# One trunk layer on one core: the first weight unit goes ahead of the next k-tiles' modulation products, and the square-root table is loaded later

## The chip, the cores and the metric

The kernel runs on one core of one Trainium2 chip. The metric is the device time of one execution in microseconds (us); lower is better. The engines are TensorE (PE for its matmuls, PEld for its weight loads), VectorE (DVE), ScalarE (ACT), GpSimd (POOL) and SyncE (SP, which here only issues DMAs).

## The reference

One layer of a diffusion trunk is applied to 128 context tokens and 256 latent tokens (384 rows of width 2048, float32). What matters here is its beginning and the place where the second half starts:

```python
sh1, sc1, g1, sh2, sc2, g2 = split(silu(cond) @ w_mod + b_mod, 6)   # one cond for context, one for latent
h  = rms_norm(x, n1) * (1 + sc1) + sh1
p  = h @ w_in                                   # 2048 -> 4096: q, k, v, u
...
x  = x + g1 * ((g_na * na + g_fn * fn) @ w_o)   # gates from h, attention and Fourier branches
h2 = rms_norm(x, n2) * (1 + sc2) + sh2
x  = x + g2 * (silu(b) * a) @ w_down            # a, b = split(h2 @ w_gate_up)
```

Each of the six pieces of the modulation is 2048 wide and needs a 2048 x 2048 part of `w_mod` (16.8 MB).

## The kernel before, in words

**Weight units.** All weights stream through one list of units, each of two k-tiles (256 rows) by 512 columns (512 KB), or one k-tile where a group has an odd one. `load_unit` (L179 on) issues the load on SyncE's queue into one of four buffers. `split_unit` makes a high part `wh` with a cast on ScalarE (L137) and a low part `wl` with a subtraction on VectorE (L138), into three buffers each, and TensorE multiplies with three matmuls for each product (`mm3`, L141 to L143). `next_unit` (L202) is called once for each unit, ahead of its matmuls: it splits a later unit, then gives one tick to every helper in the list `behind` (and to those in `front`, which get two there and one more from `mid_unit`), then issues another load.

**Helpers and rates.** A helper is a Python generator wrapped in `Paced` (L54). A tick adds its `rate` to `due`, and each whole 1 in `due` runs the generator on to its next `yield`, which I call a step. The engines' instructions are thus put into their queues in an order that these counts set. Each engine takes its own queue strictly in order; engines wait for each other by semaphores.

**The opening.** `x` is loaded, transposed and squared, and `mod_cols` (L358 on) makes shift and scale 1 in column form: it loads `w_mod` in chunks of 1 MB (tile `wm`, three buffers), multiplies each chunk with the conditions (32, 16 or 8 matmuls into tile `md`, at 128, 256 or 512 columns), and asks for the chunk three ahead. It does so for the k-tiles in the parts `MODS`: 0; 1 to 2; 3 to 6; 7 to 10; 11 to 14; 15. Then `modulate(kt)` (L520) makes `hH`, `hL` of one k-tile. The input projection runs in four groups (`GROUPS`), so that it can begin before all k-tiles are there: k-tile 0 alone, 1 to 2, 3 to 6, 7 to 15; in each, eight column chunks of 512 (8, 8, 16 and 40 units). All that comes after k-tile 0 is one helper, `prep` (L548 to L559): for a part of n k-tiles 2n chunk steps, 3 more (the last chunk's step also copies the products; one step does nothing, one turns them with matmuls at L405, one adds the bias at L415 to L418), and n steps of `modulate`. At the start of a group `prep.due` is set to `DUE` and its rate to `PREP` (L623):

```python
DUE = [0, -0.5, 0, 0]
PREP = [1.3, 1.8, 2.3, 2.3]
RATES = [1.455, 0.5, 1.1, 0.937, 0.452]
```

A group's matmuls also force `prep` on if the k-tile that they need has not been modulated yet (L632).

**The other four pieces.** When `prep` has ended, its `then` (L577) appends the helper `rows` to `behind`; its first tick comes with the next unit. `rows` (L562) makes pieces 2 (gate 1), 4 (scale 2), 3 (shift 2) and 5 (gate 2) in this order: multiply-adds on VectorE (L312, L314), then a sum over partitions with matmuls (L324), an addition of the bias on VectorE (`row`, L329), and four small stores from GpSimd's queue to DRAM (`s_row`, L334). For pieces 4 and 3 `columns` reads the row back as columns (`colr`, L340, two loads on GpSimd's queue), transposes it on TensorE (L347), and writes it to `msc[1]` or `msh[1]` on VectorE (L351 for shift 2). The rates of `rows` are those of `RATES`: 1.455 in the input projection, 0.5 for each of three ticks of a unit in the gate stage (64 units), 1.1 in the branch projections (32 units), 0.937 in the output projection, where it is set to 0 for the last two of 32 units. Where a piece must be there, `rows_until(ty)` (L573) runs the steps that are still missing, on the spot.

**The end of the output projection.** After its last unit the sums of squares are reduced and `inv_sqrt` runs (L1149 to L1152), then `rows_until(3)` (L1153), then TensorE transposes the reciprocal roots (L1157), ScalarE copies them (`rB`, L1159) and `normed` makes the first k-tiles of `h2` for the feed-forward stage.

**Activation tables.** `warm_sqrt` (L145) is a one-column square root, so that ScalarE loads the table of roots there and not where the real root (L157) waits.

Of the kernel before, what the change touches and what calls it, by code (L numbers as in the profile page):

```python
# [38 lines left out]
MODS = [(0, 1), (1, 2), (3, 4), (7, 4), (11, 4), (15, 1)]  # L39
GROUPS = MODS[:3] + [(7, 9)]  # L40
ORDER = [6, 7, 0, 1, 2, 3, 4, 5]
DUE = [0, -0.5, 0, 0]
PREP = [1.3, 1.8, 2.3, 2.3]
PAIR = "qk,b,pv,s0 m0,e0 i0,,s1 m1,e1 i1,,t0,v,,t1,,"
RATES = [1.455, 0.5, 1.1, 0.937, 0.452]
# [50 lines left out]
def trunk_kernel(ctx: ExitStack, tc: tile.TileContext, io: dict):  # L96
# [35 lines left out]
    def nm(s):  # L132
        return f"{s}{next(ids)}"
# [11 lines left out]
    def warm_sqrt():  # L145

        warm = small.tile([P, 1], F32, tag="warm", bufs=1, name=nm("warm"))
        nc.scalar.activation(out=warm, in_=ones[:, 0:1], func=AF.Sqrt)
# [112 lines left out]
    with ExitStack() as ph:  # L261
# [7 lines left out]
        def at_tile():  # L269
            return pa.tile([P, CH], F32, tag="at", name=nm("at"))  # L270
# [3 lines left out]
        def acc_tile():  # L274

            return next(ring)()
# [147 lines left out]
        with ExitStack() as pha:  # L424
# [4 lines left out]
            def c6(shape, name):  # L429
                return cpool.tile(shape, F32, tag="c6", name=nm(name))  # L430
# [39 lines left out]
            nc.scalar.activation(  # L470
                out=csz[:, :, 0:2], in_=pt[:, 0:32].rearrange("p (c k) -> p k c", c=2), func=AF.Silu
            )
            warm_sqrt()


            ssx = small.tile([P, NT, 4], F32, tag="ssx", bufs=1, name="ssx")
# [1 line left out]
            for cc in range(4):  # L478
                xT.append(c6([P, 4, TOK], "xT"))
                for k in range(4):  # L480
                    o = acc_tile()
                    for t in (1, 2, 0):
                        nc.tensor.transpose(o[:, t * P : (t + 1) * P], xc[cc][:, t, k * P : (k + 1) * P], ident)
                    nc.vector.tensor_copy(xT[cc][:, k], o[:, :TOK])
                for t in (1, 2, 0):
                    junk = tmp.tile([P, CH], F32, tag="junk", bufs=1, name=nm("junk"))
                    nc.scalar.activation(
                        out=junk, in_=xc[cc][:, t], func=AF.Square, accum_out=ssx[:, t, cc : cc + 1]
                    )
                if cc == 1:  # L490
                    pt = at_tile()
                    nc.tensor.transpose(pt[:, 0:64], rows_n, ident[:64, :64])
                    nc.vector.tensor_copy(ng, pt[:, 0:32].rearrange("p (i k) -> p i k", i=2))
                    nc.vector.tensor_copy(bcol, pt[:, 32:64])
                    nc.vector.tensor_scalar_mul(qg8, qg[:, 0:1], HD**-0.5)
            ss1 = small.tile([P, NT], F32, tag="ss1", bufs=1, name="ss1")
            nc.vector.tensor_reduce(out=ss1, in_=ssx, axis=AX.X, op=ALU.add)
            r1 = small.tile([P, NT], F32, tag="r1", bufs=1, name="r1")
# [123 lines left out]
            for gi, (k0, n) in enumerate(GROUPS):  # L622
                prep.due, prep.rate = DUE[gi], PREP[gi]  # L623
                if gi == len(GROUPS) - 1:
# [700 lines left out]
```

## Time and profile before

| | us |
|---|---|
| median of 3 runs | 2071.12 (2070.62 to 2074.38) |
| the profiled execution, its time | 2071.76 |
| its span, first to last instruction | 2070.0 |
| TensorE matmuls busy | 2035.2 (98%) |
| VectorE busy | 1225.5 (59%) |
| ScalarE busy | 758.2 (37%) |
| GpSimd busy | 43.2 (2%) |
| mean granted TensorE clock | 0.996 of full speed |

The profile is of one execution. Times in its rows count from the first instruction, so that 1.76 us of the execution lie outside the span. Busy time of TensorE runs on while a matmul waits in the pipeline; idle time before an instruction stands in brackets with the engine and line that released it. The page of the profile gives the whole execution in groups; the timeline gives the instructions of one engine in order of time, merged where neighbours are alike.

### The profile page before, as it was taken

The numbers are of one execution on the slowest core, as the hardware profiler recorded it, in microseconds if no ns is written. First come the engines' busy times: TensorE is split into PE (matmuls) and PEld (weight loads), VectorE is DVE, ScalarE is ACT, GpSimd is POOL, SyncE is SP. The second block draws the span as 40 slices with busy tenths as digits, with TensorE's granted clock in tenths as the row PEclk, the third lists the DMA queues.
The fourth block names the chain that finished last, engine by engine and source line by source line (L and its number), as shares of the span: only waits on it lengthen the run. The fifth ranks groups of instructions, "written<-read, shape, count | busy, mean of one in ns | idle before, by whom it ended". The sixth has DMA issues, their size and how long they took to land.

```text
span 2070.0 us, 27406 instructions
## 1 busy us (share of the span) xinstructions
PE 2035.2 (98%) x10986; PEld 1846.1 (89%) x10986; DVE 1225.5 (59%) x1454; ACT 758.2 (37%) x1133; POOL 43.2 (2%) x92
## 2 busy tenths in 40 slices
PE   7999999999999999998999999999999999999999
PEld 4658888999999999887998899899989998999897
DVE  5635899688986787765554444544454434333456
ACT  5323232456665443334433332223222232223222
POOL 1000000000001000001000000000000000000000
PEclk9999999999999999999999999999999999999999
DMA  9887878677774775754545554455454444444453
GB/s 329 297 318 218 298 247 315 209 211 232 213 223 150 255 245 198 244 182 133 153 153 163 157 159 153 136 160 162 154 163 133 125 130 127 128 126 128 130 166 122
DMA packets 219999, 390.45 MB, mean 189 GB/s; under 512 B 28080, under 2 KB 64960, under 8 KB 219872
## 3 DMA queue, kind: packets, MB, share of 16 engines
q1 hardware_dynamic: 212704, 382.13, 58.2%
q10 hardware_dynamic: 4672, 6.31, 0.8%
q8 instruction: 86, 1.41, 0.3%
q0 software_dynamic: 2496, 0.27, 0.1%
q14 instruction: 41, 0.34, 0.0%
HBM read 371.81 MB, written 20.51 MB: 190 GB/s over the span
## 4 chain that ended last, share of the span: by engine, by line
PE 89%; DVE 3%; DMA 3%; ACT 2%; issue 1%; SPq 1%; ACTq 0%; DVEq 0%
PE mm L141 18%; PE mm L143 18%; PE mm L142 18%; PE at L143 11%; PE at L141 11%; PE at L142 10%; PE md L392 1%; DMA wm<-in_w_mod 1%; DVE accr L314 1%; DMA wraw<-in_w_gate 1%; DVE wl L138 1%; ACT wh L137 0%; ACT sc L900 0%; SPq L368 0%; PE at L858 0%
## 5 line engine op out<-in xcount | busy, mean ns | idle before, releaser
L138 DVE TENSOR_TENSOR wl<-wraw,wh 128x1024 fp32r<-128x1024 f32 (+1 forms) x464 | 559.1, 1205 | 699.9 <-ACT wh L137 693.5
L137 ACT CAST wh<-wraw 128x1024 fp32r<-128x1024 f32 (+1 forms) x464 | 480.6, 1037 | 1030.3 <-PE at L142 283.5
L141 PE MATMUL mm<-hH,wh 128*128 128x384 f32 x1216 | 411.6, 338 | 3.6 <-ACT gst L998 2.5
L143 PE MATMUL mm<-hH,wl 128*128 128x384 f32 x1216 | 407.6, 335 | 0.0
L142 PE MATMUL mm<-hL,wh 128*128 128x384 f32 x1216 | 407.2, 335 | 0.0
L314 DVE SCALAR_TENSOR_TENSOR accr<-wmr,csz,accr 128x1024 f32<-128x1024 f32 x240 | 304.7, 1277 | 0.1
L141 PE MATMUL at<-hH,wh 128*128 128x384 f32 x704 | 236.6, 336 | 1.4 <-ACT hH L1170 1.4
L141 PEld LDWEIGHTS mm<-hH,wh 128*128 128x128 f32 x1216 | 228.9, 188 | 9.2 <-ACT gst L998 3.7
L142 PE MATMUL at<-hL,wh 128*128 128x384 f32 x704 | 236.4, 336 | 0.0
L143 PE MATMUL at<-hH,wl 128*128 128x384 f32 x704 | 235.9, 335 | 0.0
L142 PEld LDWEIGHTS mm<-hL,wh 128*128 128x128 f32 x1216 | 229.0, 188 | 0.0
L143 PEld LDWEIGHTS mm<-hH,wl 128*128 128x128 f32 x1216 | 228.7, 188 | 0.0
L141 PE MATMUL mm<-wh,hH 128*128 128x512 f32 x422 | 168.8, 400 | 1.8 <-DVE gl L1054 1.2
L142 PE MATMUL mm<-wl,hH 128*128 128x512 f32 x422 | 165.0, 391 | 0.9 <-DVE wl L138 0.9
L143 PE MATMUL mm<-wh,hL 128*128 128x512 f32 x422 | 164.7, 390 | 0.0
L143 PE MATMUL mm<-wh,cL 128*128 128x512 f32 x352 | 137.1, 389 | 0.0
L141 PE MATMUL mm<-wh,cH 128*128 128x512 f32 x352 | 137.0, 389 | 0.0
L142 PE MATMUL mm<-wl,cH 128*128 128x512 f32 x352 | 137.0, 389 | 0.0
L141 PEld LDWEIGHTS at<-hH,wh 128*128 128x128 f32 x704 | 132.7, 189 | 2.8 <-ACT hH L1170 1.8
L142 PEld LDWEIGHTS at<-hL,wh 128*128 128x128 f32 x704 | 132.7, 189 | 1.1 <-DVE hL L1176 0.7
L143 PEld LDWEIGHTS at<-hH,wl 128*128 128x128 f32 x704 | 132.7, 189 | 0.0
L141 PEld LDWEIGHTS mm<-wh,hH 128*128 128x128 f32 x422 | 79.5, 188 | 33.7 <-issue 11.1
(239 smaller groups left out, 2390.2 us busy)
## 6 DMA issues: line engine op xcount, KB each, us to landing
wraw<-in_w_gate_up SPq DMA_DIRECT2D x176, 512.0 KB, 3.7
wmr<-in_w_mod SPq DMA_DIRECT2D x128, 512.0 KB, 4.2
wraw<-in_w_down SPq DMA_DIRECT2D x88, 512.0 KB, 3.7
wm<-in_w_mod SPq DMA_DIRECT2D x64, 512.0 KB, 7.1
wraw<-in_w_gate SPq DMA_DIRECT2D x64, 512.0 KB, 5.0
wraw<-in_w_in SPq DMA_DIRECT2D x56, 512.0 KB, 5.8
wraw<-in_w_o SPq DMA_DIRECT2D x32, 512.0 KB, 5.5
wraw<-in_w_fnet_proj SPq DMA_DIRECT2D x16, 512.0 KB, 6.2
```

Of the source, the lines that this page charges most:

```text
L137: nc.scalar.copy(H, x)
L138: nc.vector.tensor_sub(L, x, fr(H))
L141: nc.tensor.matmul(out, aH, bH, start=start, stop=False)
L142: nc.tensor.matmul(out, aH, bL, start=False, stop=False)
L143: nc.tensor.matmul(out, aL, bH, start=False, stop=stop)
L314: nc.vector.scalar_tensor_tensor(out=acc[:, cnd], in0=wm, scalar=sc, in1=acc[:, cnd], op0=ALU.mult, op1=ALU.add)
L392: nc.tensor.matmul(pm[q : q + 32, :w], csz[:, k, :], wm[:, ty, kk + par, :], start=k < 2, stop=k >= KT - 2, tile_position=(0, q), skip_gro ...
```

## The change

`DUE` of the first group goes from 0 to -1.4, so that `prep` gets no step with the first unit and one step fewer in the first group. `warm_sqrt` moves from behind the SiLU of the conditions to behind the squares of the third column chunk of `x`. Nothing else differs.

```diff
-DUE = [0, -0.5, 0, 0]
+DUE = [-1.4, -0.5, 0, 0]
 PREP = [1.3, 1.8, 2.3, 2.3]
...
                 out=csz[:, :, 0:2], in_=pt[:, 0:32].rearrange("p (c k) -> p k c", c=2), func=AF.Silu
             )
-            warm_sqrt()
...
                     nc.vector.tensor_scalar_mul(qg8, qg[:, 0:1], HD**-0.5)
+                if cc == 2:
+                    warm_sqrt()
             ss1 = small.tile([P, NT], F32, tag="ss1", bufs=1, name="ss1")
```

## Rows read from the trace of the kernel before

**Rows 1.** The page, busy time, share of the span and instructions of TensorE.

```profile
PE 2035.2 (98%) x10986; PEld 1846.1 (89%) x10986; DVE 1225.5 (59%) x1454; ACT 758.2 (37%) x1133; POOL 43.2 (2%) x92
```

**Rows 2.** The timeline, TensorE, opening: start us, busy us, engine, line, operation, [idle before].

```profile
22.22 1.07 PE L392 MATMUL md<-wm,csz 128*32 128x128 f32 x28 [1.32 <-DMA wm<-in_w_mod]
...
26.23 1.07 PE L392 MATMUL md<-wm,csz 128*32 128x256 f32 x4 [2.19 <-DVE hL L534]
...
35.81 1.07 PE L392 MATMUL md<-wm,csz 128*32 128x256 f32 x16
...
39.07 1.07 PE L392 MATMUL md<-wm,csz 128*32 128x256 f32 x16
...
51.51 0.50 PE L141 MATMUL mm<-wh,hH 128*128 128x512 f32 x1 [0.56 <-ACT acc L644]
```

**Rows 3.** Windows: us; busy PE, PEld, DVE, ACT, POOL; granted clock; DMA share; GB/s.

```profile
30.00:31.00 1.00, 1.00 (x4) 0.73 (x3) 0.00 (x0) 0.00 (x0) 0.00 (x0) 0.50 1.07 358
31.00:32.00 1.00, 1.00 (x6) 0.83 (x5) 0.00 (x0) 0.65 (x2) 0.00 (x0) 0.92 1.10 352
```

**Rows 4.** The timeline, ScalarE, opening.

```profile
5.97 1.28 ACT L148 ACT_TABLE_LOAD   x1
...
14.15 0.63 ACT L487 ACTIVATE junk<-xc 128x512 f32<-128x512 f32 x1
...
48.01 0.99 ACT L537 ACTIVATE hf<-xT,msh,msc 128x128 f32<-128x128 f32 x2
49.03 0.51 ACT L137 CAST hH<-hf 128x384 fp32r<-128x384 f32 x1
```

**Rows 5.** The timeline, SyncE's queue, opening: DMA issues.

```profile
27.35 3.16 SPq L368 DMA_DIRECT2D wm<-in_w_mod  x4
```

**Rows 6.** The timeline, TensorE, 112 to 156 us: modulation chunks.

```profile
112.91 2.54 PE L392 MATMUL md<-wm,csz 128*32 128x512 f32 x16
...
117.09 1.05 PE L392 MATMUL md<-wm,csz 128*32 128x512 f32 x4 [0.29 <-DMA wm<-in_w_mod]
...
148.47 1.07 PE L392 MATMUL md<-wm,csz 128*32 128x512 f32 x8
...
154.10 1.05 PE L392 MATMUL md<-wm,csz 128*32 128x512 f32 x4 [0.30 <-DMA wm<-in_w_mod]
```

**Rows 7.** The timeline, SyncE's queue, start of the last group.

```profile
187.25 0.68 SPq L245 DMA_DIRECT2D s_rpb<-in_rpb  x1
...
192.23 1.92 SPq L289 DMA_DIRECT2D wmr<-in_w_mod  x3
```

**Rows 8.** The timeline, VectorE, output projection.

```profile
887.07 1.23 DVE L138 TENSOR_TENSOR wl<-wraw,wh 128x1024 fp32r<-128x1024 f32 x1 [1.66 <-ACT wh L137]
...
944.58 0.68 DVE L329 TENSOR_TENSOR row<-row,md 128x512 f32<-128x512 f32 x1
...
962.99 0.18 DVE L351 COPY msh<-md 128x32 f32<-128x32 f32 x1
```

**Rows 9.** The timeline, GpSimd: the two row stores that columns are read from.

```profile
647.55 1.91 POOL L334 DMA_DIRECT2D s_row<-row  x4 [119.55 <-DVE row L329]
...
651.25 0.48 POOL L340 DMA_DIRECT2D colr<-s_row  x1 [0.65 <-DMA s_row<-row]
...
945.55 1.91 POOL L334 DMA_DIRECT2D s_row<-row  x4 [143.80 <-DVE row L329]
949.34 0.99 POOL L340 DMA_DIRECT2D colr<-s_row  x2 [1.88 <-DMA s_row<-row]
```

**Rows 10.** DMA issues at 645 to 655, then 940 to 965 us: last number, us to landing.

```profile
colr<-s_row POOLq DMA_DIRECT2D x2, 8.0 KB, 2.1
...
colr<-s_row POOLq DMA_DIRECT2D x2, 8.0 KB, 3.5
```

**Rows 11.** The timeline, TensorE, end of the output projection.

```profile
963.13 0.90 PE L1157 MATMUL mm<-ident,r 128*128 128x128 f32 x3 [3.58 <-DVE r L162]
```

**Rows 12.** Windows of 1 us, same columns as Rows 3, end of the output projection.

```profile
963.00:964.00 1.00, 0.87 (x4) 0.87 (x5) 0.17 (x2) 0.00 (x0) 0.00 (x0) 0.50 0.00 0
```


## The prediction

> **What bounds the kernel now.** The page comes first: TensorE's matmuls are busy for 98% of the span [rows 1], so the end moves by what TensorE loses or gains in waits, wherever the change reaches. Two places are to be read: the opening, which the change edits, and every later place that counts steps from it. About 0.2% (4.1 us) is what a measurement of this kernel can tell from no change.
>
> In the timeline of the opening TensorE waits for the second chunk of k-tile 0 until 22.22, and starts again at 26.23, when the first `hL` is there [rows 2]. What it starts is not the first unit but the first chunk of k-tiles 1 and 2, which stands ahead of the unit in its queue; the clock stands at half (1.2 GHz), because TensorE had hardly worked since 23.3, and comes back about 31.16: the window from 30 is granted 0.50, the next 0.92 [rows 3]. Further on, unit 7 loses 0.56 us to ScalarE, which copies sums late because it modulates k-tiles 1 and 2 just then [rows 2, 4].
>
> **Part 1: the first unit ahead.** With -1.4 + 1.3 = -0.1, `prep` gets no step in unit 0. From 26.23 to 35.81 TensorE did two chunks and two units. At full clock one chunk with one unit takes 39.07 - 35.81 = 3.26 us, both pairs 6.52 us; they took 9.58, so 3.06 us went to the half clock and to waits for the chunk's data [rows 2]. In the new order the unit's operands are all there at 26.23, and the chunk's data are there before the unit is over. If the clock comes back at the same 31.16, the 4.93 us before it do 2.46 us' worth, and the other 4.06 us end at 35.22: a gain of 0.6. At full clock throughout it would be 3.06, and 0 at least, since the same work starts at the same time. I take 1.0, near the lower end, because nothing makes TensorE warmer at 26.23 than it was.
>
> The modulations of k-tiles 1 and 2 move from unit 6 to unit 7, one unit ahead of their use. On ScalarE they are a cast of about 1.06, then twice 0.99 and 0.51 [rows 4], 4.06 us together; TensorE has a unit (2.26), a chunk (1.0) and a first k-tile (0.7) to do meanwhile, 3.96. So the stall of 0.56 goes, and one of about 0.1, with the subtraction behind it up to 0.6, may come: gain 0.3, ends -0.5 and 0.56.
>
> On SyncE's queue the next weight load no longer stands behind four halves of chunks whose issue took 3.16 us for want of a buffer [rows 5]; the chunks go out after it, within 1 us. Their use is a unit later as well, so that costs nothing; without that unit of cover a chunk would be late by the issue, under 1 us. GpSimd's queue gets nothing moved in the opening.
>
> **Part 2: the streams of k-tiles 7 to 14.** Every `prep` step comes one step later. In units 17 to 20 the eight chunks of 7 to 10 now fall as 2, 2, 3, 1, which is how those of 11 to 14 fell in units 23 to 26; these in turn now fall as 1, 2, 3, 2, where before 7 to 10 fell as 1, 2, 2, 3. Three chunks in a row stall on loads: 112.91 to 118.14 is 5.2 us for three chunks of 1.0, a loss of 2.2; 148.47 to 155.15 is 6.7, a loss of 3.7 [rows 6]. The first stream takes the second's pattern and about the other way round, because the last two chunks are still asked for three units after the first. I take 0, ends -1.5 and +1.5 (both at 3.7, both at 2.2).
>
> **Part 3: the table.** Without the load at 5.97 (1.28 us) the squares begin earlier, nine of them done by about 12.8 (0.75 each); the load and the warm-up fill the time until the last chunk of `x`, whose squares began at 14.15 [rows 4]. They begin at about 14.2 again. Cost 0. Its cover: the root feeds `rB`, and TensorE waits for a load until 22.22 in any case [rows 2]; if that were gone it would cost up to 1.4 us.
>
> **Part 4: the other pieces, one unit later.** `prep` needs 61 calls to end: 9 + 15 + 15 + 15 + 6 steps and the one that ends it. Before, the groups gave 10 (1.3 x 8), 13 (-0.5 + 1.8 x 8) and 36 (2.3 x 16), and the first unit of the last group 2: it ended there. Now they give 9, 13, 36 and 2, so it ends in the second unit, and `rows` starts one unit later. The trace agrees for before: the bias expansion, one load a unit, begins at 187.25, and the first loads of `rows` follow in the second unit at 192.23 [rows 7]. That gave 39 ticks x 1.455 = 56.745; 64 x 3 x 0.5 = 96; 32 x 1.1 = 35.2; 30 x 0.937 = 28.11; together 216.055. A check: the sum crosses no whole number only in unit 15 of the output projection (202.002 to 202.94), and the split of that unit is the one with no multiply-add behind it [rows 8]. With one tick less it is 214.6.
>
> A piece stops 69 times in `mod_rows`; with its columns and its end, pieces 2 and 4 take 70 and 75 steps. For piece 3 step 214 is the sum over partitions, 215 the bias addition with the four stores, 216 the column loads, 219 the transpose, 220 the copy. Before, 215 came in unit 28 (944.58) [rows 8], the round trip through DRAM ran beside three units of matmuls, and only 217 to 220 were left to `rows_until(3)`. Now 215 is left to it too, and so **the addition stands on VectorE's queue behind the whole of the last unit and `inv_sqrt`**, although its operands have long been there. Behind it stand, in order: stores, loads, the transpose on TensorE's queue, and behind that the transposes of the roots, `rB` and all of the feed-forward stage.
>
> The chain: the addition begins where the copy began, at 962.99, and takes 0.68 [rows 8], to 963.67. First store 0.29 later (945.55 against 944.58 + 0.68) [rows 8, 9], 963.96. From the first store to the second column load it took 651.25 - 647.55 = 3.70, or 949.34 + 0.49 - 945.55 = 4.28 [rows 9]; that load lands in 2.1, or 3.5 [rows 10]. The shorter ones ran with little weight traffic, the longer beside 512 KB loads; here the DMA share is 0.00 [rows 12], so I take 3.70 + 2.1: 969.76, and 0.25 for the transpose: 970.0. The roots' transposes began at 963.13 [rows 11]. **Cost 6.9 us**, ends 6.8 and 8.9. The clock adds nothing: it was at half in the window from 963 already [rows 12].
>
> A store's landing here, inside the 3.70, is 651.25 - (647.55 + 3 x 0.48) = 2.26 us. The Trainium skill, "DMA: Bandwidth & Descriptors", section "Anatomy of one DMA", gives about 2.0 us fixed for each DMA, most of it the wait until the write is confirmed, longest for HBM. This speaks against the change: two such costs in a row become visible. By it the two would be 4.0 and not 4.36, and the sum 0.4 us lower; the trace agrees within that.
>
> **Sum.** -1.0 - 0.3 + 0 + 0 + 6.9 = +5.6 us. The profiled execution would go from 2071.76 to 2077.4; it stands 0.64 above the median, so the forecast is 2076.7.
>
> **Rivals.** (a) *The tail is free*: the addition is still put in front of the last residual, as if `rows` had started in the same unit. Then only the opening counts: 2071.1 - 1.3 = 2069.8, not slower. It decides at the count: 215 must be reached within 30 units. For it: only 0.4 of a step is missing, and a helper that I count wrongly by one tick would do. Against: the check at unit 15 fixes the sum within 0.06. 0.08. (b) *The streams are freed*: with other spacing the chunks of k-tiles 7 to 14 arrive in time and most of the 5.9 us lost there comes back (say 4): 2072.7. For it: loads are asked for at other times; against: the same three-unit dependence. 0.06. (c) *The opening gives nothing*, because the half clock covers the first unit wholly and unit 8 waits for its modulations: 2071.1 + 6.9 = 2078.0. 0.06. The forecast itself has 0.80.
>
> **How the numbers follow.** The forecast's own range is +3.9 (6.8 less a gain of 2.9) to +8.9: 2075.0 to 2080.0. With (c) inside it, 0.86 lies there; I stretch the lower end to 2074.2 for the streams. Slower by over 0.2% is above 2075.3: nearly all of the forecast (0.77) and (c), 0.83. Within: (a) 0.07, the rest of the forecast and most of (b), 0.14. Faster by over 0.2%: 0.03.
>
> **What would show it.** Right: the first matmul on L141 at about 26.2 and the modulation chunk behind it; the first `wmr` loads one unit later against the bias expansion; the last `row` addition before the feed-forward stage behind the last `inv_sqrt`; TensorE's transposes on L1157 beginning about 10 us after the last unit's matmuls and not 3.6, released by a DMA through L347. Wrong: that addition still among the last units, or L347 without a wait; or three-chunk rows that end without a wait for `wm`; or an opening that is 4 us shorter.

## The result, and the profile after

| | before | after |
|---|---|---|
| median, us | 2071.12 (2070.62 to 2074.38) | 2080.24 (2079.48 to 2083.29) |
| profiled execution, us | 2071.76 | 2080.07 |
| its span, us | 2070.0 | 2078.3 |
| mean granted clock | 0.996 | 0.993 |

The ratio is 1.0049 [1.0038, 1.0059]: the change costs 9.1 us, where 5.6 were forecast. The sign is the forecast one and the median lies 0.24 above the upper end of the range. The work is the same: TensorE is busy for the same time in the same number of matmuls as in [rows 1], and the span is 8.3 longer. From the page of the kernel after, the busy times and the chain that ended last:

```profile
PE 2034.8 (98%) x10986; PEld 1848.6 (89%) x10986; DVE 1226.3 (59%) x1454; ACT 758.0 (36%) x1133; POOL 43.3 (2%) x92
...
PE 86%; DVE 5%; ACT 3%; DMA 3%; issue 2%; SPq 1%; ACTq 0%; POOL 0%; DVEq 0%; POOLq 0%
```

So the loss is in waits, and the list of waits on TensorE says where (engine, tile and line that waited, what for: us in total, times, the longest):

```profile
PE md L347 <- DMA colr<-s_row: 10.7, 2, 10.4
...
PE mm L141 <- DVE acc L649: 4.2, 1, 4.2
```

Three places make up the difference, in order of time. "Lead" and "behind" below compare the start of each matmul in one trace with the start of the same matmul in the trace before.

**The opening gained 4.2 us in this execution.** TensorE's timeline, to be held against [rows 2]:

```profile
26.31 0.79 PE L141 MATMUL mm<-wh,hH 128*128 128x512 f32 x1 [1.23 <-ACT hH L534]
...
30.52 1.07 PE L392 MATMUL md<-wm,csz 128*32 128x256 f32 x16
...
33.79 1.07 PE L392 MATMUL md<-wm,csz 128*32 128x256 f32 x16
```

The unit stands ahead of the chunk. Two units and two chunks run from 26.31 to the end of the second chunk at about 34.8: 8.5 us, where they took 9.58. No wait stands at unit 7 any more (0.56 in [rows 2]). In the streams of k-tiles 7 to 14 the rows of three chunks, to be held against [rows 6], are:

```profile
110.14 2.01 PE L392 MATMUL md<-wm,csz 128*32 128x512 f32 x16
...
113.80 1.05 PE L392 MATMUL md<-wm,csz 128*32 128x512 f32 x4 [0.29 <-DMA wm<-in_w_mod]
...
144.95 1.92 PE L392 MATMUL md<-wm,csz 128*32 128x512 f32 x16
...
148.73 1.05 PE L392 MATMUL md<-wm,csz 128*32 128x512 f32 x4 [0.35 <-DMA wm<-in_w_mod]
```

4.7 and 4.8 us, for 3.0 of work each: 3.5 lost, where before 2.2 + 3.7 = 5.9 were. The gains add up to 1.1 + 0.56 + 2.4 = 4.1. SyncE's queue shows the lead at the start of the last group (187.25 in [rows 7]), and that the first loads of `rows` come with the third bias expansion and no longer with the second:

```profile
183.03 0.67 SPq L245 DMA_DIRECT2D s_rpb<-in_rpb  x1
...
192.11 1.77 SPq L289 DMA_DIRECT2D wmr<-in_w_mod  x3
```

**Near 340 us the lead is lost.** There the input projection ends and the gate stage begins. TensorE's timeline of the kernel after:

```profile
324.86 0.50 PE L142 MATMUL mm<-wl,hH 128*128 128x512 f32 x1 [1.55 <-DVE wl L138]
...
341.46 0.69 PE L141 MATMUL mm<-hH,wh 128*128 128x384 f32 x1 [4.22 <-DVE acc L649]
```

The same two matmuls in the kernel before:

```profile
328.13 0.50 PE L142 MATMUL mm<-wl,hH 128*128 128x512 f32 x1 [0.35 <-DVE wl L138]
...
341.61 0.44 PE L141 MATMUL mm<-hH,wh 128*128 128x384 f32 x1 [1.10 <-DVE acc L648]
```

A window of 5 us, of the kernel after and then of the kernel before (columns as in [rows 3]):

```profile
340.00:345.00 5.00, 3.54 (x13) 3.54 (x14) 5.00 (x7) 0.00 (x0) 0.00 (x0) 0.66 0.72 231
...
340.00:345.00 5.00, 3.90 (x22) 3.58 (x22) 5.00 (x7) 2.10 (x2) 0.00 (x0) 1.00 1.00 375
```

The first wait is 1.2 longer and the second 3.1; about 1.1, the rest of the 5.4, is put down to the matmuls at half clock behind it. Held matmul by matmul against the trace before, the kernel after is 4.2 ahead until 322 us and 1.2 behind from 345 us on. It falls further back inside the gate stage, to 4.9 at 532 us, and is at 1.1 again from the output projection on. Most of that fall (3.5) comes at a wait on the gate's operands at 513.90 (1.96, with the clock at 0.50 from 515 to 518). Part of the way back is that before such a wait stood at 648.50 (2.20, with the clock at 0.50 from 649 to 652), where the kernel after has 0.58 at 650.65.

**The end of the output projection loses 6.9 us**, as forecast. Three timelines of the kernel after answer to [rows 8, 9, 11]. VectorE:

```profile
964.00 0.16 DVE L162 SCALAR_TENSOR_TENSOR r<-rst,rss 128x3 f32<-128x3 f32 x1
964.40 0.69 DVE L329 TENSOR_TENSOR row<-row,md 128x512 f32<-128x512 f32 x1 [0.24 <-issue]
```

and the first of these operations in the kernel before:

```profile
962.91 0.16 DVE L162 SCALAR_TENSOR_TENSOR r<-rst,rss 128x3 f32<-128x3 f32 x1
```

GpSimd, the stores and the loads:

```profile
965.38 1.92 POOL L334 DMA_DIRECT2D s_row<-row  x4 [150.81 <-DVE row L329]
967.96 0.49 POOL L340 DMA_DIRECT2D colr<-s_row  x1 [0.66 <-DMA s_row<-row]
968.93 0.49 POOL L340 DMA_DIRECT2D colr<-s_row  x1 [0.49 <-DMA s_row<-row]
```

TensorE, the transposes of the columns and of the roots:

```profile
970.90 0.28 PE L347 MATMUL md<-ident,colr 32*128 32x32 f32 x1 [10.44 <-DMA colr<-s_row]
971.11 0.90 PE L1158 MATMUL mm<-ident,r 128*128 128x128 f32 x3
```

The addition stands behind the last operation of `inv_sqrt`, the stores behind it, the loads behind these. The roots' transposes begin at 971.11 and not at 963.13: 7.98 later, of which 1.09 is lag that was there already (`r` at 964.00, and at 962.91 before).

The account is -4.2 + 5.4 + 6.9 = +8.1, for a span that is 8.3 longer. What made the loss near 340 us, and what each part is worth in medians, the runs had to tell.

### The profile page after: what moved, and what is told of

Read it like the earlier page. It is cut to its first block, busy times and chain, and to the rows that moved or that the text cites. A ratio compares the mean times of both kernels' runs of the same rounds, so it can differ in the third digit from the quotient of the medians.

```text
span 2078.3 us, 27409 instructions
## 1 busy us (share of the span) xinstructions
PE 2034.8 (98%) x10986; PEld 1848.6 (89%) x10986; DVE 1226.3 (59%) x1454; ACT 758.0 (36%) x1133; POOL 43.3 (2%) x92
## 4 chain that ended last, share of the span: by engine, by line
PE 86%; DVE 5%; ACT 3%; DMA 3%; issue 2%; SPq 1%; ACTq 0%; POOL 0%; DVEq 0%; POOLq 0%
PE mm L141 18%; PE mm L143 17%; PE mm L142 17%; PE at L141 10%; PE at L143 10%; PE at L142 10%; DVE accr L314 1%; PE md L392 1%; DVE wl L138 1%; DMA wm<-in_w_mod 1%; DMA wraw<-in_w_gate 1%; ACT sc L911 1%; ACT wh L137 1%; ACT sc L901 1%; DMA wmr<-in_w_mod 0%
```

## The experiments

Line numbers in the diffs are left out; ratios and differences are to the kernel before, measured beside each experiment. Each ratio's interval is about 0.1% (2 us) to either side, so that a difference between two experiments is known to 2 or 3 us.

**1. The tail taken out** (on the kernel after):

```diff
-RATES = [1.455, 0.5, 1.1, 0.937, 0.452]
+RATES = [1.455, 0.5, 1.1, 0.99, 0.452]
```

> The changed kernel with the output projection's rate at 0.99 and not 0.937, so that step 215 (the addition) and 216 fall within its last units again: 55.29 + 96 + 35.2 + 29.7 = 216.2. Theory (the lost step costs the round trip): the wait of 10.4 us on L347 goes, TensorE's transposes of the roots begin 3.6 us after the last unit again, and the time falls by 7 to 8 us, to 1 to 2 us above the kernel before. Rival (the end of the output projection waits for something else as well, or the longer time comes mostly from the place near 340 us): falls by under 4 us.

Measured: 2074.79, ratio 1.0019 [1.001, 1.0028]; the kernel before had 2070.99. In TensorE's timeline the wait on L347 is gone, and the roots' transposes wait 3.58 as in [rows 11]:

```profile
962.99 0.25 PE L347 MATMUL md<-ident,colr 32*128 32x32 f32 x1
966.82 0.54 PE L1158 MATMUL mm<-ident,r 128*128 128x128 f32 x3 [3.58 <-DVE r L162]
```

But the kernel is still 3.8 slower than before, and the wait near 340 us is still there, at 3.75. The time fell by 5.3, between the 7 to 8 of the theory and the rival's under 4. So the DRAM round trip is real, and it is not the whole loss.

**2. `rows` given back the tick that it lost** (on the kernel after; the helper then starts with 1.455 in `due`, so that after its first tick, one unit late, it stands where it stood before, unit for unit):

```diff
-rows = Paced(rows_and_columns(), RATES[0])
+rows = Paced(rows_and_columns(), RATES[0], -1)
```

> The changed kernel, but the helper of the other four pieces starts with 1.455 in its due, so that from its second tick on it stands where it stood before, unit for unit. Both theories: the tail is as before. Theory A (from 245 to 345 us VectorE and the loads are full, so the 4.2 us that the opening gains are absorbed there whatever the phase): the lead over the kernel before is gone at 345 us, and the whole time is within 1.5 us of the kernel before. Theory B (the loss near 340 us comes from the shifted steps, two multiply-adds in the last unit where before there was one): the lead of 4 us stays to the end, 2067 against 2071.

Measured: 2069.24, ratio 0.9989 [0.998, 0.9998]. Neither the tail nor the wait near 340 us (0.61 there) is left. What remains is the opening: 1.75 us to the good (0.4 to 4 by the interval). That is between the two theories, which had asked for at most 1.5 and for 4; and since the lead in this execution was only 0.4 at 322 us, it can't show what becomes of a lead of 4. It does show that both losses hang on the one tick that `rows` is late.

**3. The late tick alone** (on the kernel before, with its old opening and table):

```diff
-rows = Paced(rows_and_columns(), RATES[0])
+rows = Paced(rows_and_columns(), RATES[0], 1)
```

> The kernel before with one edit: the helper of the other four pieces starts with -1.455 in its due, one tick late, as the change makes it. Opening as before. Theory of the tail: plus 7 to 8 us, TensorE waiting about 10 us on L347. For the place near 340 us: theory A (VectorE and loads full) says no loss there, as VectorE has 1.5 steps (1.9 us) less to do, so plus 5 to 8 in all; theory B (shifted steps) says 3 to 5 us more are lost there, plus 10 to 13 in all.

Measured: 2083.61, ratio 1.0059 [1.0046, 1.0072]: 12.6 us slower with no lead to absorb, so theory A falls and B stands: by the matching matmuls 6.0 are lost between 322 and 345 us, and 7.1 at the end of the output projection. Since it differs from before in nothing but the place of `rows` in the queues, its rows near 340 us show the cause. First the timelines of the kernel before. SyncE's queue:

```profile
326.96 0.33 SPq L595 DMA_DIRECT2D s_qkvu<-acc  x1
327.34 0.62 SPq L597 DMA_DIRECT2D out_new_v<-acc  x1
328.10 1.07 SPq L181 DMA_DIRECT2D wraw<-in_w_gate  x1
331.62 0.33 SPq L289 DMA_DIRECT2D wmr<-in_w_mod  x1
```

ScalarE, the cast of the gate's first weights:

```profile
337.45 1.05 ACT L137 CAST wh<-wraw 128x1024 fp32r<-128x1024 f32 x1 [4.08 <-DMA wraw<-in_w_gate]
```

VectorE, from their split to the sums:

```profile
338.53 1.23 DVE L138 TENSOR_TENSOR wl<-wraw,wh 128x1024 fp32r<-128x1024 f32 x1 [0.41 <-ACT wh L137]
339.68 1.28 DVE L314 SCALAR_TENSOR_TENSOR accr<-wmr,csz,accr 128x1024 f32<-128x1024 f32 x1
340.87 1.28 DVE L648 TENSOR_TENSOR acc<-acc,mm 128x512 f32<-128x512 f32 x2
```

Then the timelines of experiment 3, `rows` one unit late. SyncE's queue:

```profile
330.37 0.33 SPq L289 DMA_DIRECT2D wmr<-in_w_mod  x1
330.75 0.42 SPq L595 DMA_DIRECT2D s_qkvu<-acc  x1
331.22 0.42 SPq L597 DMA_DIRECT2D out_new_v<-acc  x1
331.74 1.36 SPq L181 DMA_DIRECT2D wraw<-in_w_gate  x1
```

ScalarE, the same cast:

```profile
339.85 1.05 ACT L137 CAST wh<-wraw 128x1024 fp32r<-128x1024 f32 x1 [5.41 <-DMA wraw<-in_w_gate]
```

VectorE, the multiply-add that frees the buffer, and the same stretch as above:

```profile
329.06 1.28 DVE L314 SCALAR_TENSOR_TENSOR accr<-wmr,csz,accr 128x1024 f32<-128x1024 f32 x1
...
340.94 1.23 DVE L138 TENSOR_TENSOR wl<-wraw,wh 128x1024 fp32r<-128x1024 f32 x1 [2.94 <-ACT wh L137]
342.08 2.47 DVE L314 SCALAR_TENSOR_TENSOR accr<-wmr,csz,accr 128x1024 f32<-128x1024 f32 x2
344.47 1.28 DVE L648 TENSOR_TENSOR acc<-acc,mm 128x512 f32<-128x512 f32 x2
```

TensorE, near 345 us (its wait on L347 at the end of the output projection is 10.47):

```profile
345.21 0.69 PE L141 MATMUL mm<-hH,wh 128*128 128x384 f32 x1 [3.63 <-DVE acc L648]
```

A `wmr` load now stands ahead of two stores and of the gate's first weights. It goes out at 330.37, when the multiply-add that frees its buffer ends (329.06 + 1.28 = 330.34), and SyncE can't pass it: the weights are asked for at 331.74 instead of 328.10, 3.6 later, and split 2.4 later. On VectorE the sums of the last chunk, which TensorE waits for, stand behind that split and behind two multiply-adds instead of one, 1.2 more: they begin 3.6 later. The Trainium skill, "DMA: Bandwidth & Descriptors", section "Anatomy of one DMA", says that a DMA's wait on a semaphore happens on the issuing sequencer, before dispatch; the rows at 330.37 to 331.74 agree.

The kernel after has the same order. On SyncE's queue:

```profile
326.03 0.33 SPq L289 DMA_DIRECT2D wmr<-in_w_mod  x1
...
327.40 2.72 SPq L181 DMA_DIRECT2D wraw<-in_w_gate  x2
```

and on VectorE the multiply-add that frees the buffer, which ends at 326.00:

```profile
324.72 1.28 DVE L314 SCALAR_TENSOR_TENSOR accr<-wmr,csz,accr 128x1024 f32<-128x1024 f32 x1
```

Before, the weights were asked for at 328.10, which the lead of 4.2 would have made 323.9: they go out 3.5 later than that.

**4. `rows` slower in the input projection, faster in the gate stage** (on the kernel after):

```diff
-RATES = [1.455, 0.5, 1.1, 0.937, 0.452]
+RATES = [1.2, 0.56, 1.1, 0.937, 0.452]
```

> The changed kernel with rates 1.2 (input projection) and 0.56 (gate stage) and not 1.455 and 0.5: 45.6 + 107.5 + 35.2 + 28.1 = 216.4 steps, so the tail is as before, and VectorE has some 10 multiply-adds (12 us) less to do in the input projection, and some 512 KB loads fewer stand beside the weights. Theory A: the lead of 4 us passes 345 us, and the time is 2066 to 2068, unless the gate stage takes it back. Theory B: with another phase again, no more than 1 us better than the kernel before.

Measured: 2078.76, ratio 1.0038 [1.0025, 1.005]. The expectation was missed. The wait near 340 us is indeed gone, but the gate stage gives the gain back, and another piece's columns come late too. From the list of waits on TensorE, and from its timeline:

```profile
PE at L859 <- DVE aT L958: 3.9, 3, 1.8
...
664.23 0.28 PE L347 MATMUL md<-ident,colr 32*128 32x32 f32 x1 [4.69 <-DMA colr<-s_row]
```

TensorE waits on `aT` from VectorE, into whose queue the moved steps now put their multiply-adds (that these are the cause was not tested); and the round trip of [rows 9], which was covered at 647 us, shows on TensorE as soon as nothing is left between.

**5. The table's move alone** (on the kernel before: `warm_sqrt` moved as in the change, and nothing else).

> The kernel before with the square-root table's warm-up moved behind the third chunk's squares, and nothing else. All theories: no change, within 0.1% (the load fills the wait for the last chunk of x). Rival: the second load or the later root delays the first modulation, plus 1 to 1.5 us.

Measured: 2070.91, ratio 1.0 [0.9991, 1.0009].

**6. The `wmr` loads on GpSimd's queue** (on the kernel after, in `mod_rows`):

```diff
-                nc.sync.dma_start(
+                nc.gpsimd.dma_start(
```

> The changed kernel with the 512 KB loads of the other four pieces issued on GpSimd's queue and not on SyncE's. Steps as in the changed kernel, so the tail stays (about 10 us of wait on L347). Theory Q (near 340 us a load of these pieces waits on SyncE's queue for a buffer that VectorE has not yet freed, and the weight loads behind it go out 3 to 4 us late): the wait of 3.6 to 4.2 us on the sums goes to about 1 us or less, and the time falls by 4 to 5 us, to 2075 to 2076. Theory V (the two multiply-adds that now stand ahead of the last unit's sums on VectorE's queue): the wait stays, the time falls by under 1.5 us.

Measured: 2078.23, ratio 1.003 [1.0019, 1.0042]. TensorE near 341 us:

```profile
341.18 0.44 PE L141 MATMUL mm<-hH,wh 128*128 128x384 f32 x1 [1.78 <-DVE acc L649]
```

The wait falls from 4.22 to 1.78; the 1.6 on `wl` stays, and the clock still falls a little later. By the matching matmuls this kernel loses 3.2 between 322 and 345 us, where the kernel after lost 5.4. So both theories hold a part: the wait on SyncE's queue makes some 2.2 us of the loss, and the other place of the multiply-adds on VectorE should make the rest, which experiment 9 tests. In all the time fell by 2.5, not by the 4 to 5 of the one theory. The same page of the Trainium skill, section "Issuing engines are not separate DMA queues", holds that issuing from several engines saves only the sequencer's time, usually little. Here it saved more than the 0.33 of an issue, some 2.2, since that time held a wait for a buffer.

**7. Both: GpSimd's queue, and the lost tick given back** (experiments 2 and 6 together).

> The changed kernel with the helper's due started at 1.455 (as in the run that kept the steps) and its 512 KB loads on GpSimd's queue. No tail. Theory Q: the wait of about 1 us at 341 us goes as well and the weights are never held up by these loads, so 2067 to 2069, a little better than the run that kept the steps. Rival: GpSimd's descriptors cost VectorE or the loads more than the queue gives back, 2070 or more.

Measured: 2067.94 (2066.01 to 2071.67), ratio 0.9983 [0.9974, 0.9992], against 2071.57 for the kernel before. The time came as expected, but not by the expected way: in the profiled execution the wait at 341 us did not go (1.20, and 1.10 in the kernel before), though that execution was also the slowest of the eleven. It has the lowest median of the study and beats both kernels; whether it also beats experiment 2 (0.9989) these intervals do not tell.

**8. The tail alone** (experiment 2, with the output projection's rate lowered until the addition is left over again):

```diff
-RATES = [1.455, 0.5, 1.1, 0.937, 0.452]
+RATES = [1.455, 0.5, 1.1, 0.88, 0.452]
```

> The changed kernel with the helper's due started at 1.455 and the output projection's rate at 0.88: 187.9 + 26.4 = 214.3 steps, so the phase up to the branch projections is that of the kernel before and only the addition and the column loads fall behind the last unit again. Theory: plus 7 us (6.9 of round trip, up to 0.5 of half clock) on the run that kept the steps, that is 2076 to 2077, with a wait of about 10 us on L347. Rival (the tail costs what the whole shift cost, 11 us): 2080.

Measured: 2075.2, ratio 1.0018 [1.0009, 1.0027]: 3.6 above the kernel before, where experiment 2 was 1.75 below its own. The round trip costs 5.4 us in medians, less than the 7 expected; by the matching matmuls of the two profiles it costs 6.9. Its row:

```profile
966.32 0.28 PE L347 MATMUL md<-ident,colr 32*128 32x32 f32 x1 [10.45 <-DMA colr<-s_row]
```

**9. Steps paused where they hurt** (experiment 6, with no steps of `rows` in the last three units of the input projection, made up for in the gate stage):

```diff
-RATES = [1.455, 0.5, 1.1, 0.937, 0.452]
+RATES = [1.455, 0.5227, 1.1, 0.937, 0.452]
...
+                        if gi == len(GROUPS) - 1 and ci == ORDER[-1] and u == k0 + n - 5:
+                            rows.rate = 0
```

> The changed kernel with the loads of the other four pieces on GpSimd's queue, and with their helper at rate 0 in the last three units of the input projection (its rate in the gate stage is 0.5227 and not 0.5, which gives the same 214.6 steps in the end). The tail stays. If what was left of the loss near 340 us with the loads on GpSimd's queue (a wait of 1.8 us on the sums, 1.6 us on the low part, and the half clock after them) is the multiply-adds ahead of splits and sums on VectorE's queue, both waits go and the time is 3 us lower than with the loads moved alone, about 2075. If it is the weight loads themselves, it stays within 1 us.

Measured: 2078.16, ratio 1.0037 [1.0024, 1.0049]. The expected time was missed, though the local effect came. TensorE near 341 us:

```profile
340.74 0.44 PE L141 MATMUL mm<-hH,wh 128*128 128x384 f32 x1 [0.66 <-DVE acc L651]
```

The matmul starts 0.87 earlier than before (341.61), and the clock stays at 1.00 behind it. VectorE's queue:

```profile
338.86 1.23 DVE L138 TENSOR_TENSOR wl<-wraw,wh 128x1024 fp32r<-128x1024 f32 x1 [4.66 <-ACT wh L137]
340.00 1.28 DVE L651 TENSOR_TENSOR acc<-acc,mm 128x512 f32<-128x512 f32 x2
```

The sums stand directly behind the split, with no multiply-add between. The pause also stops the loads of `rows` (the last goes out at 329.12), but the weights come no earlier for that: their cast starts at 337.78, after a wait of 4.83 for them, and in experiment 6 it started at 335.83. So the multiply-adds, and not the loads, were the rest of the loss on the sums. The wait on `wl`, which was expected to go too, is still there (1.54 at 327.68, ahead of the pause). But what was won there is lost by the end of the output projection. From the timeline of VectorE, where `r` stood at 962.91 before:

```profile
965.43 0.16 DVE L162 SCALAR_TENSOR_TENSOR r<-rst,rss 128x3 f32<-128x3 f32 x1
```

0.87 ahead has become 2.5 behind. The list of waits shows a part of it, 4.1 us on the gate's operands (L1001) instead of 2.5. The paused steps come in the gate stage, whose order was set for other steps; which of them does the harm there was not taken apart.

**10. The same pause on experiment 7.**

> The same two edits on the kernel that kept the steps (due started at 1.455): no tail, no wait at 341 us. 2066 to 2068, and no worse than the run with GpSimd's queue alone (2067.9).

Measured: 2070.36, ratio 1.0 [0.9991, 1.0009], against 2070.95. The expected 2066 to 2068 was missed: the wait at 341 us is gone, but the gate stage takes the gain back. By the matching matmuls it is 4.7 ahead of before at 385 us and 0.2 behind at 532, where experiment 7 goes through the same stretch without a change (0.3 behind, then 0.1 ahead). So experiment 7 keeps the lowest median: the rates of before fit the gate stage, and the other places of these steps that were tried (experiments 4, 9 and 10) cost there what they saved near 340 us, or more.

## Why the prediction was right, and where it was wrong

**Part 1, the opening: right.** The mechanism and the size held, and the sign of being wrong, an opening that is 4 us shorter, did not come: 9.58 - 8.5 = 1.1 for a forecast of 1.0, and the clock came back a little earlier than the 31.16 it was reckoned with, since the window from 30 to 31 was granted 0.82. Unit 7's stall went in this execution (0.56); in experiment 2's it came back as 0.8 and 0.2 on `hH`, so that the forecast's 0.3, between ends of both signs, was fair. All that is left of the change in experiment 2 is worth 1.75 in medians; 1.3 was forecast for the opening.

**Part 2, the streams: right in the pattern, outside its ends in this execution.** The patterns of two and three chunks a unit came as counted and three chunks in a row still waited, but 2.4 us came back, more than the 1.5 allowed. Much of that is this execution's own, since others of the same opening had no lead at the end of it: see the last section.

**Part 3, the table: right.** ScalarE's timeline, for [rows 4]:

```profile
12.67 1.28 ACT L148 ACT_TABLE_LOAD   x1
```

The load runs in the gap before the last chunk of `x` (TensorE waits for that chunk until 13.68), whose squares begin at 14.07 where they began at 14.15. Experiment 5 measures no change (within 0.09%).

**Part 4, the tail: right, nearly to the row.** The count was right: step 215 was left to `rows_until(3)`. (The sum at unit 15 of the output projection is 202.000 and not 202.002, which changes nothing.) From the addition's start to the roots' transposes it took 971.11 - 964.40 = 6.7, where 7.0 was forecast: 3.55 from the first store to the second load (968.93 - 965.38) and 1.97 until the transpose were each a little shorter. The choice of the shorter trip was right, though its reason, little weight traffic, is doubtful: the DMA share was 0.48 to 0.58 from 648 to 653 us, and in the tail itself at most 0.04. The cost was 6.9 in the profile, as forecast; that it agrees to the digit is luck, since the addition also began 0.3 later than `r` had led to expect. In the profiles of the five kernels that have this tail it is 6.6 to 7.2 by the matching matmuls, and in medians it is measured twice, at 5.4 (experiment 8 against 2) and 5.3 (the kernel after against experiment 1). "The clock adds nothing" holds within 0.3: the lag is 8.0 at the transposes and 8.3 from 980 us on. The Trainium skill's rule of about 2.0 us for each DMA ("DMA: Bandwidth & Descriptors", "Anatomy of one DMA") agrees as well: the load took 1.97.

**The step that failed** is also in Part 4. It counted `rows` one unit late by its steps alone, put what the shift does on the way at nothing without a reason, and looked for the consequence only where a step crosses out of a stage. But the steps in between put something into two queues: `wmr` loads on SyncE's, multiply-adds on VectorE's. One unit late, all of them stand at other places among weight loads, splits and sums for the whole stage. From the start of the last group to 322 us that costs nothing: the lead stays at 4.2. It costs at the end of the input projection, where TensorE waited before already: VectorE is busy without a gap in the window from 340 us on (5.00 of 5 us, in both kernels), and the gate's first weights come only just then (their cast waited 4.08 for them before). There it cost 5.4 us in the profile of the kernel after. In medians the late tick with the tail covered costs 5.55 (experiment 1 is 3.80 above the kernel before, experiment 2 1.75 below). That figure is of the whole kernel: in experiment 1's profile 5.2 are lost between 322 and 345 us and 1.7 of them are won back by 955.

With it the sum closes: -1.75 + 5.55 + 5.4 = +9.2, measured +9.1. Experiment 3, where nothing of the opening is gained, should then lose 11.0; it lost 12.6, so that a term is good to 1 or 2 us, and that the sum closes to 0.1 is chance. The range's upper end of 2080.0 was the forecast's own with the dearest tail (8.9), and had no term for a shift of `rows` elsewhere. None of the three rivals had one either. (a) falls by the rows at the tail; of (b) a part came in this execution, 2.4 of its 4, but not on its own; (c) asked for an opening that gives nothing, and it gave 1.75.

## What to carry to other kernels

When a helper's start moves by one unit, walk every queue it issues into through the whole stage, not only the place where its last step lands: look for the spots where a critical load or sum stands right behind one of its instructions on an in-order queue, above all at a change of stage. Look there too for loads that wait for a buffer: on SyncE's queue they held up the weights behind them, and issuing them from GpSimd was worth some 2.2 us where the steps were late, and nothing measurable where they were not. And after changing where a paced helper starts, set its counts back to what the tuned rates were made for (here one argument, worth 11 us), before judging the change itself.

## What the runs showed of the hardware

The opening's lead is not a property of the code alone. With the same opening as the kernel after, the first bias expansion of the last group was issued at 183.03, 187.48, 186.83, 183.99, 185.16, 187.48, 184.78, 185.85 and 184.12 (the kernel after, and experiments 1, 2, 4 and 6 to 10); with the old one at 187.25, 187.36 and 187.49. On average that is a lead of 2.0 (187.4 against 185.4), but single executions show anything from 4.3 to none. Only a part of that is there from the first loads of `x`: the first unit began at 26.31 in the kernel after and at 27.66 in experiment 2, but at 25.95 in experiment 1, whose bias expansion came as late as with the old opening. One profile could not have told the worth of the opening; the medians tell it to within 2 us.

A wait of TensorE cost more than its length where the clock fell behind it. In the kernel after the clock is granted at 0.50, which is 1.2 GHz, from 341 to 344 us, behind the wait of 4.22; in experiments 1 and 6 it falls about a microsecond after the work has begun again (waits of 3.75 and 1.78); in the kernel before and in experiments 7 and 9 (1.10, 1.20 and 0.66) it stays at 1.00. In the kernel after that cost about 1.1, by what the waits leave of the loss.

Loads of 512 KB issued from GpSimd landed later than from SyncE (a median of 5.1 us from issue in experiment 7, 4.4 in experiment 2) and took longer to issue (0.53 and 0.34), but cost the kernel nothing that could be measured here (ratios 0.9983 and 0.9989).
